# Another choice of the quads whose operand sets are stored ahead of the down projection

## The chip, the cores and the metric

The kernel runs on one core of one Trainium2 chip. The metric is the time of one execution on the device in microseconds (us); the median of several runs is compared. A second number is the span of one execution that the hardware profiler recorded, from which all views below come. Engines: PE is TensorE (matmul), DVE is VectorE, ACT is ScalarE, POOL is GpSimd, SP is SyncE, which issues nearly all transfers here and waits in its order for what each of them needs.

## The reference

One decoder layer in float32 for 256 tokens of width 2048. What matters here is its second half, a gated feed-forward net of width 5632:

```
x = x + concat(attention, pooling) @ w_out
h = rms_norm(x, g)
u = h @ w_up                              # 2048 -> 2 * 5632
y = conv_b + sum of conv_w[i] * u shifted by 2-i tokens, i = 0..2
gate, val = split(y)
out = x + (silu(gate) * val) @ w_down     # 5632 -> 2048
```

## The kernel before

All weights are read once, in 1 MB chunks of 128 x 2048 float32, through four buffers (`raw`). The program is a list of steps; a step uses half a chunk (128 x 1024), so chunk c serves steps 2c and 2c + 1. Each float32 operand is split into a high part `wh` (ACT, L165) and a low part `wl` (DVE, L170), and three matmuls (high x high, high x low, low x high) stand for one exact one. The split of a step is made five steps ahead of its use (`AHEAD`), and when the last split of a chunk is made, its buffer goes to the next load (`release`, L139). The order of all instructions is the order of the program; nothing reorders them.

The feed-forward net is done in thirds of 8, 8 and 6 groups of 256 hidden features. Each third has an up projection (8 steps a group, into `ps_feat`; the convolution and gate follow on DVE, ACT and POOL) and then a down projection over the third's hidden features, made as two pairs (`down_pair`): pair 0 makes output columns 0 to 1023, pair 1 columns 1024 to 2047. A pair has 8 or 6 quads of two steps; quad j uses steps 2j and 2j + 1 of its pair. `MIXED` names for each pair the quads that are made with seven block products in place of eight, in the manner of Strassen and Winograd. A mixed quad needs sums of weight blocks: DVE forms them (L189, L190, L191), and ACT and DVE split them (L211, L213, L224) into an operand set of two tiles `s1` and `s4` (together 128 x 3072, 1.5 MB), and a third sum, t13, is split as an ordinary half chunk.

There are two buffers for sets. Set 0 lies in memory that is kept. Set 1 lies in the memory of the temporaries of the convolution (`temps`), and is opened by `open_temps(True)` in step 2 of a third's pair 0; the last operation that reads one of those temporaries is L761, in the same step. `SECOND` names the quads that use set 1, the other mixed ones use set 0. In pair 0 of the last third the partial results of the mixed quads are taken out of PSUM behind the last mixed quad by `add_part`'s L927, L905, L906 and L910; in the other pairs by L918 to L927.

Two quads of each third do not have their set made in the down projection. Their chunk is loaded once more in the up projection (`extra`, L143), the set is formed there in set 0's memory, and set and t13 are stored to HBM (`early_store`, L204 and L205). In the down projection t13 comes with the chunk's other half (L136, L137), and the set is loaded by `load_set` (L208), `ahead` steps ahead of the quad's first step. `STORED` names these quads by third size, as (pair, quad, ahead):

```
MIXED = {8: ((0, 3, 5, 6), (0, 3, 5, 6)), 6: ((0, 3, 4), (0, 2, 3))}
SECOND = {8: ((5,), (0, 3, 6)), 6: ((4,), (2,))}
STORED = {8: ((0, 6, 4), (1, 5, 6)), 6: ((1, 2, 6), (1, 3, 4))}
...
        for i, (b, j, ahead) in enumerate(STORED[nq]):
            u = u0 + 8 * nq + b * 2 * nq + 2 * j
            at = u0 + 22 + 2 * nq * i - 4 * i * (nq < 8)
            extra[(at + 4) // 2] = u // 2
            after(at, early_sums)
            after(at + 1, early_split)
            after(at + 3, lambda c=u // 2: early_store(c))
            after(u - ahead, lambda c=u // 2, i=int(j in SECOND[nq][b]): load_set(c, i))
```

`after(u, f)` runs f behind step u. In most steps the splits (and so the release of a chunk and the next load) stand ahead of the step's matmuls, and the functions of `after` behind them.

Of the kernel before, what the change touches and what calls it, by code (L numbers as in the profile page):

```python
# [56 lines left out]
THIRDS = ((0, 8), (8, 16), (16, 22))  # L57
MIXED = {8: ((0, 3, 5, 6), (0, 3, 5, 6)), 6: ((0, 3, 4), (0, 2, 3))}
SECOND = {8: ((5,), (0, 3, 6)), 6: ((4,), (2,))}
STORED = {8: ((0, 6, 4), (1, 5, 6)), 6: ((1, 2, 6), (1, 3, 4))}  # L60
SUMMED = {n: sorted(set(a + b)) for n, (a, b) in MIXED.items()}
OUT_MIXED = (2, 3, 5, 6)
OUT_SECOND = (3, 6)
# [25 lines left out]
def layer(ctx: ExitStack, tc: tile.TileContext, xT, xtok, wts, par, rel_d, ident_d, icnt_d, out):  # L89
# [991 lines left out]
    for n, (g0, g1) in enumerate(THIRDS):  # L1081
        nq, u0 = g1 - g0, len(steps)
        for i, (b, j, ahead) in enumerate(STORED[nq]):
            u = u0 + 8 * nq + b * 2 * nq + 2 * j
# [133 lines left out]
```

## Time and profile before

| | |
|---|---|
| median of 3 runs | 1032.47 us (1032.01 to 1034.42) |
| profiled execution | 1034.1 us, span 1032.3 us |
| TensorE busy | 1011.9 us (98%) |
| VectorE busy | 856.8 us (83%) |
| ScalarE busy | 590.5 us (57%) |
| read from HBM, written | 211.56 MB, 15.07 MB |
| down projections (pair 0's first quad) begin at | 469.1, 736.1 and 958.1 us |

A timeline's row gives the start, the duration, the engine, the line and operation, what is written from what, and how many; in brackets stands the idle time of the engine ahead of it and what ended it. In the chain of waits, a row gives start, duration and what. A row of a table by stretches has the stretch, its length, busy time of PE, PE's weight loads, DVE, ACT and POOL, then the granted TensorE clock (1.00 is full), the share of the DMA engines' time and GB/s.

### The profile page before, as it was taken

How to read it: one execution, taken by the hardware profiler on the slowest of the kernel's cores; microseconds unless marked ns; L12 is line 12 of the kernel's file. 1: busy time of each engine (PE TensorE's matmuls, PEld its weight loads, DVE VectorE, ACT ScalarE, POOL GpSimd, SP SyncE). 2: the span in 40 equal slices, each digit the busy share in tenths (PEclk: the TensorE clock that was granted, in tenths of full speed). 3: DMA queues.
4: the chain of work that ended last, by engine and by line, in shares of the span. 5: the costliest groups of instructions: out<-in, count | busy, mean ns of one | idle time of the engine just before them, and what ended most of it. 6: DMA issues, size and time to landing. Idle time of an engine off the chain costs nothing.

```text
span 1032.3 us, 13718 instructions
## 1 busy us (share of the span) xinstructions
PE 1011.9 (98%) x5229; PEld 865.0 (84%) x5229; DVE 856.8 (83%) x1105; ACT 590.5 (57%) x803; POOL 102.5 (10%) x110
## 2 busy tenths in 40 slices
PE   9999999999999999999899999999989999999988
PEld 8788888888888888888688888888868888888766
DVE  5998767888988888889785898898987679888984
ACT  6855664565666655655455555665555465555561
POOL 0220005500001111000000111100000001110011
PEclk9999999999999999999899999999999999999999
DMA  9784553475554585845587647685476775577476
GB/s 334 283 263 177 194 184 120 163 305 183 206 201 165 204 317 185 317 168 197 224 306 221 228 172 273 216 320 200 163 284 202 290 225 183 195 290 291 163 242 207
DMA packets 36801, 233.81 MB, mean 226 GB/s; under 512 B 4264, under 2 KB 5160, under 8 KB 12416
## 3 DMA queue, kind: packets, MB, share of 16 engines
q1 hardware_dynamic: 34000, 224.15, 59.7%
q0 software_dynamic: 2736, 8.78, 4.2%
q8 instruction: 41, 0.67, 0.3%
q14 instruction: 24, 0.20, 0.1%
HBM read 211.56 MB, written 15.07 MB: 220 GB/s over the span
## 4 chain that ended last, share of the span: by engine, by line
PE 91%; DVE 4%; DMA 3%; issue 1%; ACT 1%; SPq 0%; DVEq 0%; ACTq 0%
PE ps_feat L251 33%; PE ps_feat L253 17%; PE ps_down L866 14%; PE ps_tok L238 8%; PE ps_p L806 7%; PE ps_down L806 5%; DMA s<-s 3%; PE ps_v L245 3%; DVE wl L170 2%; PE ps_pool L260 1%; PE ps_s L468 1%; ACT wh L165 0%; PE ps_start L313 0%; PE ps_down L888 0%; DVE y L735 0%
## 5 line engine op out<-in xcount | busy, mean ns | idle before, releaser
L170 DVE TENSOR_TENSOR wl<-raw,wh 128x1024 fp32r<-128x1024 f32 x358 | 441.6, 1247 | 85.2 <-ACT wh L165 28.5
L251 PE MATMUL ps_feat<-x2h,wh 128*128 128x512 f32 x1408 | 488.8, 392 | 0.0
L165 ACT ACTIVATE wh<-raw 128x1024 fp32r<-128x1024 f32 x358 | 369.2, 1051 | 123.1 <-DVE raw L189 67.7
L253 PE MATMUL ps_feat<-x2h,wl 128*128 128x256 f32 x1408 | 393.5, 280 | 0.0
L251 PEld LDWEIGHTS ps_feat<-x2h,wh 128*128 128x128 f32 x1408 | 264.2, 188 | 58.4
L253 PEld LDWEIGHTS ps_feat<-x2h,wl 128*128 128x128 f32 x1408 | 264.2, 188 | 0.1
L730 ACT ACTIVATE y<-fs,pv 128x256 f32<-128x256 f32 x88 | 48.2, 595 | 64.5 <-DVE fs L728 64.5
L735 DVE SCALAR_TENSOR_TENSOR y<-fs,pv,y 128x255 f32<-128x255 f32 (+1 forms) x176 | 81.0, 481 | 3.2
L866 PE MATMUL ps_down<-wh,hid 128*128 128x512 f32 x336 | 83.1, 389 | 0.0
L866 PEld LDWEIGHTS ps_down<-wh,hid 128*128 128x128 f32 x336 | 63.1, 188 | 13.4
L780 POOL TENSOR_TENSOR s<-y 128x128 f32<-128x128 f32 x24 | 32.6, 1358 | 349.0 <-DVE y L754 349.0
L211 ACT ACTIVATE s<-raw 128x512 fp32r<-128x512 f32 (+1 forms) x54 | 45.4, 840 | 17.5 <-DVE raw L191 14.9
L896 POOL DMA_DIRECT2D x<-st x13 | 11.5, 921 | 408.5 <-ACT st L971 329.0
L251 PE MATMUL ps_feat<-xh,wh 128*128 128x512 f32 x128 | 46.3, 402 | 0.0
L866 PE MATMUL ps_down<-wl,hid 128*128 128x512 f32 x168 | 44.9, 389 | 0.0
L520 ACT ACTIVATE fs<-ps_feat 128x512 f32<-128x512 f32 (+1 forms) x46 | 26.2, 570 | 21.8 <-PE ps_feat L253 21.8
L866 PEld LDWEIGHTS ps_down<-wl,hid 128*128 128x128 f32 x168 | 31.5, 188 | 6.6
L755 ACT ACTIVATE hid<-y 128x512 fp32r<-128x512 f32 x22 | 13.9, 634 | 38.5 <-DVE y L754 38.5
L253 PE MATMUL ps_feat<-xh,wl 128*128 128x256 f32 x128 | 35.8, 280 | 0.0
L238 PE MATMUL ps_tok<-wh,xh 128*128 128x512 f32 x128 | 35.5, 399 | 0.0
L806 PE MATMUL ps_p<-wh,sx 128*128 128x512 f32 x104 | 34.6, 415 | 0.0
L245 PE MATMUL ps_v<-wh,xh 128*128 128x512 f32 x128 | 34.5, 391 | 0.0
(240 smaller groups left out, 1271.7 us busy)
## 6 DMA issues: line engine op xcount, KB each, us to landing
raw<-in_wts SPq DMA_DIRECT2D x177, 1024.0 KB, 5.0
s<-s SPq DMA_DIRECT2D x12, 1536.0 KB, 11.6
x<-st POOLq DMA_DIRECT2D x11, 512.0 KB, 9.0
raw<-in_wts SPq DMA_DIRECT2D x10, 512.0 KB, 5.4
t<-t SPq DMA_DIRECT2D x6, 512.0 KB, 9.5
raw<-t SPq DMA_DIRECT2D x6, 512.0 KB, 5.8
x<-in_xtok SPq DMA_DIRECT2D x1, 2048.0 KB, 9.2
raw<-in_wts SPq DMA_DIRECT2D x7, 256.0 KB, 5.6
```

The costliest lines, as they stand in the source:

```text
L165: nc.scalar.activation(wparts[u][0], raw(u - 1 if u - 1 in seven else u + 1 if u in seven else u), AF.Copy)
L170: nc.vector.tensor_tensor(wl, raw(u - 1 if u - 1 in seven else u + 1 if u in seven else u), wh.bitcast(F32), op=OP.subtract)
L211: nc.scalar.activation(parts[0], w, AF.Copy)
L238: nc.tensor.matmul(ps[:, t, :], act[:, k0 + k, a, t * P:(t + 1) * P], w[:, k * 512:(k + 1) * 512], start=(first and k == 0 and n == 0), st ...
L245: nc.tensor.matmul(ps[:, t, :], act[:, k, a, t * P:(t + 1) * P], w[i], start=(first and n == 0), stop=(last and n == 2))
L251: nc.tensor.matmul(ps, wh[:, ws], act[:, k, :, :], start=(first and n == 0), stop=False, skip_group_check=True)
L253: nc.tensor.matmul(ps[:, S:], wl[:, ws], act[:, k, 0, :], start=False, stop=(last and n == len(ks) - 1), skip_group_check=True)
L730: nc.scalar.activation(y[:, m, :], u[:, m, :], AF.Identity, scale=cw[m][2], bias=col(C_CB + f0_ + m))
L735: nc.vector.scalar_tensor_tensor(y[:, m, d:], u[:, m, :S - d], cw[m][2 - d], y[:, m, d:], op0=OP.mult, op1=OP.add)
L780: eng.tensor_tensor(s[:, n, :], a, b, op=op)
L806: nc.tensor.matmul(ps, act[a], w[i], start=(first and n == 0), stop=(last and n == 2), skip_group_check=skip)
L866: nc.tensor.matmul(bank(t, b), hid(order[j] + h, t)[a], part(w, b if h == 0 else 1 - b)[i], start=(n == 0 and h == 0 and (fresh or j == no ...
```

## The change

In the thirds of eight quads, the first stored quad of pair 0 is quad 5 in place of quad 6, with its load seven steps ahead in place of four; quad 5 uses set 1, quad 6 set 0. Quad 5 of pair 1 stays stored. In the last third, quad 4 of pair 0 and quad 2 of pair 1 (both set 1) are stored, in place of quads 2 and 3 of pair 1, with loads five and six steps ahead. The sets of quad 6 (thirds of eight) and of quad 3 of pair 1 (last third) are now made in the down projection. Each engine has as many instructions as before.

```
-STORED = {8: ((0, 6, 4), (1, 5, 6)), 6: ((1, 2, 6), (1, 3, 4))}
+STORED = {8: ((0, 5, 7), (1, 5, 6)), 6: ((0, 4, 5), (1, 2, 6))}
```

SP in pair 0 of the first third, before and after: `raw` are chunks, `t` a stored t13, `s_1926` set 0, `s_4352` set 1, and `s_3315` the stored set in HBM.

```order
-L139 DMA raw<-in_wts 128x2048 x11
+L139 DMA raw<-in_wts 128x2048 x10
 L136 DMA raw<-in_wts 128x1024
 L137 DMA raw<-t_3314 128x1024
-L139 DMA raw<-in_wts 128x2048 x4
-L208 DMA s_1926<-s_3315 128x3072
 L139 DMA raw<-in_wts 128x2048 x2
+L208 DMA s_4352<-s_3315 128x3072
+L139 DMA raw<-in_wts 128x2048 x5
```

The load of the stored set has moved ahead past three chunk loads, from behind chunk 10's to behind chunk 7's (chunks counted from the pair's first), and into the other buffer. The second third changes in the same way.

SP in the last third, before; `s_8443` is set 1, `s_7554` set 0:

```order
L139 DMA raw<-in_wts 128x2048 x9
L136 DMA raw<-in_wts 128x1024
L137 DMA raw<-t_7798 128x1024
L136 DMA raw<-in_wts 128x1024
L137 DMA raw<-t_8014 128x1024
L139 DMA raw<-in_wts 128x2048
L208 DMA s_8443<-s_7799 128x3072
L139 DMA raw<-in_wts 128x2048
L208 DMA s_7554<-s_8015 128x3072
```

And after, where `s_8444` is set 1:

```order
L139 DMA raw<-in_wts 128x2048 x5
L136 DMA raw<-in_wts 128x1024
L137 DMA raw<-t_7798 128x1024
L139 DMA raw<-in_wts 128x2048 x3
L208 DMA s_8444<-s_7799 128x3072
L136 DMA raw<-in_wts 128x1024
L137 DMA raw<-t_8014 128x1024
L139 DMA raw<-in_wts 128x2048 x2
L208 DMA s_8444<-s_8015 128x3072
L139 DMA raw<-in_wts 128x2048
```

Both loads now go into set 1; the first stands behind the load of pair 1's second chunk.

DVE in the last third, from L761 (step 2 of pair 0) to the removal of pair 0's partial results, before:

```order
L761 TENSOR_TENSOR hid<-y,hid 128x2x256
L170 TENSOR_TENSOR wl<-raw,wh 128x1024
L213 TENSOR_TENSOR s_8443<-raw,s_8443 128x512
L189 TENSOR_TENSOR raw<-raw 128x1024
L190 TENSOR_TENSOR raw<-raw 128x512
L191 TENSOR_TENSOR raw<-raw 128x512
L170 TENSOR_TENSOR wl<-raw,wh 128x1024
L224 TENSOR_TENSOR s_8443<-raw,s_8443 128x1024
L170 TENSOR_TENSOR wl<-raw,wh 128x1024 x3
L213 TENSOR_TENSOR s_7554<-raw,s_7554 128x512
```

And after:

```order
L761 TENSOR_TENSOR hid<-y,hid 128x2x256
L170 TENSOR_TENSOR wl<-raw,wh 128x1024 x5
L213 TENSOR_TENSOR s_7554<-raw,s_7554 128x512
L189 TENSOR_TENSOR raw<-raw 128x1024
L190 TENSOR_TENSOR raw<-raw 128x512
L191 TENSOR_TENSOR raw<-raw 128x512
L170 TENSOR_TENSOR wl<-raw,wh 128x1024
L224 TENSOR_TENSOR s_7554<-raw,s_7554 128x1024
L170 TENSOR_TENSOR wl<-raw,wh 128x1024
L927 TENSOR_TENSOR x_1923<-ps_p_8368,x_1923 128x2x512
L906 TENSOR_TENSOR st<-ps_p,st 128x512
```

The making of quad 4's set, in `s_8443`, is gone from between the splits; the set in `s_7554` that follows is that of pair 1's first quad in both.

## The prediction

> **What bounds the kernel now.** I read the page first, then the waits, the chain, and the timelines of TensorE, VectorE and SP around each wait that the chain names. The page gives the span and TensorE's share.
>
> ```profile
> span 1032.3 us, 13718 instructions
> PE 1011.9 (98%) x5229; PEld 865.0 (84%) x5229; DVE 856.8 (83%) x1105; ACT 590.5 (57%) x803; POOL 102.5 (10%) x110
> ```
>
> TensorE is the bound; only its 20 us of idleness, and the slow clock behind a stop, can be won without touching its work. Two rows of the waits (total, times, longest) name stops inside the down projections:
>
> ```profile
> PE ps_p L806 <- DMA s<-s: 8.7, 3, 4.2
> PE ps_p L806 <- DVE st L906: 3.8, 1, 3.8
> ```
>
> Three stops wait for a load of a stored set, the first two over 3.8 us each. The chain shows why they are late (start, duration, what):
>
> ```profile
> 494.11 0.33 SPq L139
> 494.49 9.66 DMA s<-s
> ...
> 761.50 9.26 DMA s<-s
> ```
>
> The set for quad 6 of pair 0 is issued at 494.49 and lands 9.66 us later. TensorE's timeline gives what it costs; the rows are the starts of quads 5, 6 and 7 of pair 0 in the first third, of quads 5 and 7 of its pair 1 (where no stop is), and of quads 5 and 7 of pair 0 in the second third.
>
> ```profile
> 494.99 0.86 PE L806 MATMUL ps_p<-s,hid 128*128 128x512 f32 x3
> ...
> 504.20 1.65 PE L806 MATMUL ps_p<-s,hid 128*128 128x512 f32 x3 [4.19 <-DMA s<-s]
> ...
> 511.96 1.98 PE L866 MATMUL ps_down<-wh,hid 128*128 128x512 f32 x8
> ...
> 543.48 0.84 PE L806 MATMUL ps_p<-s,hid 128*128 128x512 f32 x3
> ...
> 553.10 2.00 PE L866 MATMUL ps_down<-wh,hid 128*128 128x512 f32 x8
> ...
> 761.93 0.86 PE L806 MATMUL ps_p<-s,hid 128*128 128x512 f32 x3
> ...
> 778.41 1.75 PE L866 MATMUL ps_down<-wh,hid 128*128 128x512 f32 x7
> ```
>
> Two mixed quads take 553.10 - 543.48 = 9.62 us undisturbed, 4.81 each. In pair 0 they take 511.96 - 494.99 = 16.97 and 778.41 - 761.93 = 16.48. The stop therefore costs 7.35 us in the first third and 6.86 in the second, 14.2 in all. Of the first, 4.40 is idleness (504.20 less quad 5's end, 494.99 + 4.81 = 499.80) and 2.95 slow matmuls: the granted clock (third value from the end) is 0.60 in the stretch behind it.
>
> ```profile
> 499.90:504.20 4.30, 0.11 (x2) 0.00 (x1) 4.16 (x5) 3.06 (x3) 0.00 (x0) 0.92 0.98 414
> 504.20:512.00 7.80, 7.80 (x22) 6.16 (x23) 2.93 (x4) 2.57 (x4) 0.00 (x0) 0.60 0.49 181
> ```
>
> **Part 1, the thirds of eight quads: the load is moved to quad 5.** Its buffer is set 1, which no quad of pair 0 uses before. It lies in the temporaries' memory, so its load (step 3, right behind chunk 7's) waits for their last reader, VectorE's L761. The rows give that L761 in the first and second third, chunk 7's issue (the first of the four), and the times from issue to landing of all six loads of sets:
>
> ```profile
> 482.06 0.68 DVE L761 TENSOR_TENSOR hid<-y,hid 128x512 fp32r<-128x512 f32 x1
> 749.01 0.69 DVE L761 TENSOR_TENSOR hid<-y,hid 128x512 fp32r<-128x512 f32 x1
> 482.17 12.27 SPq L139 DMA_DIRECT2D raw<-in_wts  x4
> DMA to landing us min/median/max: 8.6/9.3/10.9
> ```
>
> Issue is at 482.8 and 749.75. With the longest landing, 10.9, the sets are there at 493.7 and 760.7; quad 5 needs them at 494.99 and 761.93. The margin is 1.3 us at worst. The load now shares the DMA engines with chunk 7 ahead and chunks 8 and 9 behind: 3 x 1.05 + 1.57 = 4.72 MB. At the 414 GB/s of the row above all of it is in 11.4 us after 482.17, at 493.6, so even equal sharing doesn't make it late. I take a gain of 14.2 us.
>
> A rule of the Trainium skill speaks against this: "DMA: Bandwidth & Descriptors", section "Where 436 GB/s comes from", says that for transfers between HBM and SBUF about 358 GB/s bind. By it the 4.72 MB would take an estimated 13.2 us, the set could come at 495.4, and the sum below would be 0.8 us worse. The trace's 414 GB/s is above that limit, so I keep the row.
>
> **Part 2, quad 6's set is now made there.** The same five VectorE operations (L213, L189, L190, L191, L224) leave quad 5 and join quad 6. In the last third one such set with a split (L170) in it lies between these rows:
>
> ```profile
> 977.77 0.69 DVE L213 TENSOR_TENSOR s<-raw,s 128x512 fp32r<-128x512 f32 x1
> ...
> 983.45 3.49 DVE L170 TENSOR_TENSOR wl<-raw,wh 128x1024 fp32r<-128x1024 f32 x3
> ```
>
> That is 5.68 us with one split of 1.16, so 4.5 without. In the first third VectorE comes from L761 at 482.74, makes five splits (to 488.5) and the set (to 494.2). Quad 6 starts at 494.99 + 4.81 = 499.8, and quad 3 has left set 0 by 494.99 - 5.44 = 489.55, where quad 4 starts (an unmixed quad takes 5.44, see part 3). The cover is 5.6 us; cost 0. Bytes, DMA counts, and ACT's copies stay equal.
>
> **Part 3, the turn to pair 1.** Without the stop, quad 0 of pair 1 starts at 494.99 + 9.62 + 5.44 = 510.05 instead of 517.40 (5.44 is quad 7, 511.96 to 517.40). It overwrites the bank that L924 reads. VectorE's and ACT's rows there, and the old start:
>
> ```profile
> 503.07 1.23 DVE L224 TENSOR_TENSOR s<-raw,s 128x1024 fp32r<-128x1024 f32 x1
> 510.35 0.70 DVE L919 TENSOR_TENSOR ps_p<-ps_p,s 128x512 f32<-128x512 f32 x1 [0.63 <-ACT s L918]
> 513.15 1.22 DVE L924 TENSOR_TENSOR x<-ps_p,x 128x1024 f32<-128x1024 f32 x1
> 501.98 1.06 ACT L211 ACTIVATE s<-raw 128x1024 fp32r<-128x1024 f32 x1 [0.40 <-DVE raw L191]
> 508.07 1.06 ACT L165 ACTIVATE wh<-raw 128x1024 fp32r<-128x1024 f32 x1 [4.09 <-PE ps_p L806]
> 509.72 0.60 ACT L918 ACTIVATE s<-ps_p 128x512 f32<-128x512 f32 x1 [0.59 <-PE ps_p L806]
> 517.40 0.86 PE L806 MATMUL ps_p<-s,hid 128*128 128x512 f32 x3
> ```
>
> ACT is free at 503.04, makes two copies (1.0 each) and L918 (0.6): 505.6. VectorE is through L224 at 504.3 and a split at 505.5. L919 thus starts at 505.65, and L924 ends 513.15 + 1.22 - 510.35 = 4.02 later, at 509.7: 0.35 us before it is needed. The old slack was 3.0. I put the cost at 0, with up to 1 us in each third as the other end, since nothing is idle in this count.
>
> **Part 4, the last third.** Quad 4 of pair 0 becomes a stored one; its load stands at step 3, five steps ahead. But here VectorE is late:
>
> ```profile
> 976.03 0.69 DVE L761 TENSOR_TENSOR hid<-y,hid 128x512 fp32r<-128x512 f32 x1
> 976.81 0.63 ACT L211 ACTIVATE s<-raw 128x512 fp32r<-128x512 f32 x1 [1.01 <-DVE hid L761]
> 939.91 36.56 SPq L139 DMA_DIRECT2D raw<-in_wts  x7
> ...
> 981.10 0.86 PE L806 MATMUL ps_p<-s,hid 128*128 128x512 f32 x3
> ...
> 994.65 1.92 ACT L971 ACTIVATE st<-ps_down 128x1024 f32<-128x1024 f32 x2
> 995.61 1.65 PE L806 MATMUL ps_p<-s,hid 128*128 128x512 f32 x3 [3.79 <-DVE st L906]
> ...
> 1001.87 1.98 PE L866 MATMUL ps_down<-wh,hid 128*128 128x512 f32 x8
> ...
> 1012.96 0.97 PE L806 MATMUL ps_p<-s,hid 128*128 128x512 f32 x3 [0.63 <-DMA s<-s]
> ...
> 1018.03 5.44 PE ps_down L866 x24
> ```
>
> Set 1 is free at 976.72: ACT's first write into it waited for the same L761. Quad 4 starts at 981.10, 4.4 us later, and no set lands in under 8.6. A chunk is issued just ahead (976.14, the last of seven), as at 494.11, so I take 9.5: the set lands at 986.25, quad 4 is 5.15 us late, and the clock drops; the nearest stop in length (4.40 us) lost 2.95 by it. Quads 4 and 5 end at 986.25 + 4.81 + 5.44 + 2.95 = 999.4, where quad 0 of pair 1 used to start at 995.61.
>
> The Trainium skill, "TensorE: Matmul & The Clock Gate", Part 1 on the HAM clock gate, has the half rate end after one busy window of about 3.4 us. One such window would lose an estimated 1.7 us, and the sum below would be 1.2 us better. The trace lost 2.95 behind the stop of this length, and the row is kept.
>
> What goes in exchange: VectorE makes one set less (4.5 us) ahead of L906, the cause of the 3.79 us stop. L906 now follows quad 4's first half (986.25 + 2.4, and some 1.5 of slow clock: 990) and two of VectorE's operations, near 993 by my estimate; so that stop is gone and so is its slow clock (quad 0 took 6.26 instead of 4.81). Quad 3 of pair 1, no longer stored, loses its wait of 0.63. Its set is made once ACT has evicted pair 0's banks (1.92 us from 999.4) and made two copies, from about 1004 to 1011, before 1014.4. Pair 1's one stored set has 15 us, from quad 4's end (994) to quad 2 (1009.6). So quads 0 to 3 run through: 999.4 + 3 x 4.81 + 5.44 = 1019.3 (quad 3's end), against 1018.03 before. The last third is 1.2 us longer. Its ends: landing 8.6 and the 1.45 of clock that the 3.79 us stop cost give 1.1 shorter; 10.9 and 0.5 more of clock give 3.1 longer.
>
> **Sum.** -14.2 + 0 + 0 + 1.2 = -13.0. The profiled execution took 1034.1 (span 1032.3), so it would take 1021.1; the runs' median, 1032.47, is 1.6 below that execution, and I predict 1019.5.
>
> **Rivals.** The turn to pair 1 becomes the bound (part 3): L924 late by 1 to 2.5 us in both thirds, at full clock. For it: the slack of 0.35 us. Against it: VectorE and ACT are waiting, not working, at 508 to 510 today. It gives about 1019.5 + 3 = 1022.5. Chance 0.15.
>
> Quad 5's set is late. It decides from a landing of 12.2 us on, beyond the longest load. One late by a microsecond in both thirds gives 1021.5. A short stop keeps the clock up, as behind this one of 2.24 us:
>
> ```profile
> 964.65 0.96 PE L806 MATMUL ps_down<-s,hid 128*128 128x512 f32 x3 [2.24 <-DVE fs L524]
> 964.70:968.00 3.30, 3.30 (x15) 2.73 (x16) 3.23 (x6) 2.05 (x3) 0.00 (x0) 1.00 0.63 204
> ```
>
> Chance 0.10.
>
> The last third doesn't stop, and its old losses go: 3.8 and 1.45 at quad 0, and 1.1 at quad 3 (1018.03 less 1001.87 + 5.44 + 2 x 4.81): 1032.47 - 14.2 - 6.3 = 1012. Against it stand the 976.72 and the 8.6. Chance 0.05.
>
> Slower: SP issues in order, and a set's load that waits for its buffer holds all weight chunks behind it. If set 1 were free only 10 us after L761, sets would land near 502, and quad 5 would stop as quad 6 does now, with the last third's new stop longer by as much: about 1032.5 + 1.2 + 10 = 1043. Only from about 6 us on does this eat the gain. Against it: ACT wrote into set 1 at 976.81, 0.1 us behind L761. Chance 0.02. That the stops move without changing the time (a gain eaten at the turn and in the last third together) has 0.02.
>
> **Numbers.** The forecast has 0.66. Its own ends are 2.3 below (last third) and 1.9 + 2 above (last third, turns): 1017.2 to 1023.4. The rivals of the turn and of quad 5 lie inside that; with a little room for the base, whose runs differ by 2.4, the range is 1016.0 to 1024.0. About 0.3% (3 us) is what a measurement of this kernel can tell from no change; all cases but the last two rivals are beyond it: faster 0.95, same 0.03, slower 0.02.
>
> **What would show it.** Right: no wait of quad 6 for a set in the first two thirds, quad 5 to quad 7 in 9.6 to 9.7 us, the granted clock at 1.00 there; set 1's load issued within 0.2 us of L761; one new stop of about 5 us at quad 4 in the last third, with slow matmuls behind it, and none for L906. Wrong: a stop at the start of pair 1 with VectorE's L924 or L927 as releaser, a stop at quad 5, or SP held at the set's load while chunks are wanted.

## The result, and the profile after

The changed kernel takes 1019.0 us (median of 4 runs, 1017.68 to 1019.69), the kernel before 1032.59 us on the same chip (4 runs, 1032.01 to 1034.42). The ratio is 0.9864, with a 95% interval from 0.9847 to 0.9881: by it 14 us less (12.3 to 15.8). The forecast was 1019.5. The profiled execution took 1018.5 us.

The page's first lines, to be laid beside those of before:

```profile
span 1016.7 us, 13717 instructions
PE 1007.4 (99%) x5229; PEld 863.0 (85%) x5229; DVE 855.8 (84%) x1105; ACT 589.0 (58%) x803; POOL 102.4 (10%) x110
```

The span is 15.6 us shorter, and only 4.5 of that is TensorE's busy time (1011.9 to 1007.4); the rest was idleness. The waits of TensorE in the down projections (total, times, longest):

```profile
PE ps_down L806 <- DVE fs L524: 2.2, 1, 2.2
...
PE ps_p L806 <- DMA s<-s: 1.9, 1, 1.9
```

Of three waits for a stored set, 8.7 us together, one is left with 1.9 us. The one for L906 (3.8 us) is gone. The one for L524, inside the last third's first quad, was there before with the same 2.2 us.

TensorE's timeline has the starts of quads 5, 6 and 7 of pair 0 and of pair 1's first quad in the first third, then those of quads 5, 6 and 7 in the second:

```profile
494.80 0.86 PE L806 MATMUL ps_p<-s,hid 128*128 128x512 f32 x3
...
499.66 0.85 PE L806 MATMUL ps_p<-s,hid 128*128 128x512 f32 x3
...
504.44 1.98 PE L866 MATMUL ps_down<-wh,hid 128*128 128x512 f32 x8
...
509.88 0.86 PE L806 MATMUL ps_p<-s,hid 128*128 128x512 f32 x3
...
754.41 0.86 PE L806 MATMUL ps_p<-s,hid 128*128 128x512 f32 x3
...
759.27 0.85 PE L806 MATMUL ps_p<-s,hid 128*128 128x512 f32 x3
...
764.05 1.98 PE L866 MATMUL ps_down<-wh,hid 128*128 128x512 f32 x8
```

No row has a bracket: nothing waits. Quads 5 and 6 take 504.44 - 494.80 = 9.64 us, and 764.05 - 754.41 = 9.64 again, where they took 16.97 and 16.48. The stretch behind quad 6's start has the full clock (third value from the end), where it had 0.60:

```profile
499.60:504.40 4.80, 4.80 (x22) 3.95 (x22) 4.68 (x6) 3.69 (x4) 0.00 (x0) 1.00 0.25 102
```

SP's timeline gives the issue of chunk 7 and of set 1's load in the first third; the view of L208 gives the times from issue to landing of the loads of sets:

```profile
481.98 0.33 SPq L139 DMA_DIRECT2D raw<-in_wts  x1
482.64 0.33 SPq L208 DMA_DIRECT2D s<-s  x1
```

```profile
DMA to landing us min/median/max: 7.9/9.0/10.4
```

That view has five of the six loads; the one at 482.64 is not among them, and the same load of the second third landed after 9.0 us. Even with the longest landing the set would be there at 482.64 + 10.4 = 493.0, 1.8 us ahead of quad 5.

In the last third stand the first quad (943.78), its second half behind the wait for L524 (950.26), then quads 3, 4 and 5 of pair 0 and quad 0 of pair 1:

```profile
943.78 0.86 PE L806 MATMUL ps_p<-s,hid 128*128 128x512 f32 x3
...
950.26 0.98 PE L806 MATMUL ps_down<-s,hid 128*128 128x512 f32 x3 [2.22 <-DVE fs L524]
951.08 3.27 PE L866 MATMUL ps_down<-wh,hid 128*128 128x512 f32 x8
...
963.61 0.84 PE L806 MATMUL ps_p<-s,hid 128*128 128x512 f32 x3
...
970.47 0.94 PE L806 MATMUL ps_p<-s,hid 128*128 128x512 f32 x3 [1.94 <-DMA s<-s]
...
976.96 2.00 PE L866 MATMUL ps_down<-wh,hid 128*128 128x512 f32 x8
...
982.42 0.84 PE L806 MATMUL ps_p<-s,hid 128*128 128x512 f32 x3
```

The chain of waits has the load that quad 4 waited for, and the unmixed quad that starts where quad 3 of pair 1 ends, as at 1018.03 before:

```profile
962.41 7.92 DMA s<-s
...
1002.42 5.44 PE ps_down L866 x24
```

From 943.78 to 1002.42 are 58.64 us; before it was 1018.03 - 958.14 = 59.89. (The chain puts the start of such a quad 0.16 us later than TensorE's timeline, in both profiles alike.) So in these two profiles 7.33 + 6.84 = 14.17 us went in the thirds of eight quads, 1.25 in the last third, and 0.2 ahead of them.

### The profile page after: what moved, and what is told of

Read it like the earlier page. It is cut to its first block, busy times and chain, and to the rows that moved or that the text cites. A ratio compares the mean times of both kernels' runs of the same rounds, so it can differ in the third digit from the quotient of the medians.

```text
span 1016.7 us, 13717 instructions
## 1 busy us (share of the span) xinstructions
PE 1007.4 (99%) x5229; PEld 863.0 (85%) x5229; DVE 855.8 (84%) x1105; ACT 589.0 (58%) x803; POOL 102.4 (10%) x110
## 4 chain that ended last, share of the span: by engine, by line
PE 90%; DVE 4%; DMA 3%; ACT 1%; issue 1%; SPq 0%; DVEq 0%; ACTq 0%
PE ps_feat L251 34%; PE ps_feat L253 17%; PE ps_down L866 15%; PE ps_tok L238 9%; PE ps_p L806 7%; PE ps_down L806 6%; DMA raw<-in_wts 2%; DVE wl L170 1%; DMA s<-s 1%; ACT wh L165 1%; PE ps_pool L260 1%; DVE y L735 1%; PE ps_s L468 1%; PE ps_down L888 0%; PE ps_T L455 0%
## 5 line engine op out<-in xcount | busy, mean ns | idle before, releaser
L238 PE MATMUL ps_tok<-wh,cat 128*128 128x512 f32 x128 | 34.4, 390 | 0.0
```

The source lines that it names most:

```text
L238: nc.tensor.matmul(ps[:, t, :], act[:, k0 + k, a, t * P:(t + 1) * P], w[:, k * 512:(k + 1) * 512], start=(first and k == 0 and n == 0), st ...
```

## The experiments

All change one line, `STORED`, of the kernel before. A minus line is that of the kernel before, a plus line the experiment's. Times are medians, each beside runs of the kernel before on the same chip.

**The thirds of eight quads alone.**

```
-STORED = {8: ((0, 6, 4), (1, 5, 6)), 6: ((1, 2, 6), (1, 3, 4))}
+STORED = {8: ((0, 5, 7), (1, 5, 6)), 6: ((1, 2, 6), (1, 3, 4))}
```

> The new choice in the thirds of eight quads alone; the last third stays as before. By the theory (the gain is the two stops of quad 6, 7.3 + 6.9 us) this kernel takes the 14.2 us off the kernel before: 1018.3, ratio 0.986. By the forecast's part 4 (the last third's change costs 1.2) it is 1.2 faster than the full change; by the trace of the full change (its last third is 58.5 us against 59.9 before) it is 1.4 slower than the full change. The rival, that the last third's change brings a large part of the gain, expects 1025 or more. The profile should show no wait of quad 6 for a set in the first two thirds, and the old stops in the last: about 2.2 us inside quad 0, 3.8 behind L906, 0.6 at quad 3 of pair 1.

Measured: 1018.79 us (4 runs, 1018.2 to 1019.13) against 1031.76, ratio 0.9874 (0.9861 to 0.9887): 13.0 us less, by the interval 11.7 to 14.3. Within the intervals that is the whole gain of the change. In its last third TensorE's stops are these:

```profile
948.95 0.97 PE L806 MATMUL ps_down<-s,hid 128*128 128x512 f32 x3 [2.22 <-DVE fs L524]
...
979.89 0.97 PE L806 MATMUL ps_p<-s,hid 128*128 128x512 f32 x3 [2.36 <-DVE st L906]
...
997.07 0.97 PE L806 MATMUL ps_p<-s,hid 128*128 128x512 f32 x3 [0.18 <-DMA s<-s]
```

The program there is that of before, and still the stops for L906 and for quad 3's set are shorter (2.36 against 3.79, 0.18 against 0.63). TensorE came to pair 1 35.1 us behind the first quad's start (979.89 - 2.36 - 942.46), and 33.7 before (995.61 - 3.79 - 958.14), while L906 let it go at the same 37.4 to 37.5. The repeats below show what had held it up.

**The last third alone.**

```
-STORED = {8: ((0, 6, 4), (1, 5, 6)), 6: ((1, 2, 6), (1, 3, 4))}
+STORED = {8: ((0, 6, 4), (1, 5, 6)), 6: ((0, 4, 5), (1, 2, 6))}
```

> The new choice in the last third alone; the thirds of eight stay as before. The forecast's part 4 expects 1.2 us more than before: 1033.7, ratio 1.001. The trace of the full change expects 1.4 us less: 1031.2, ratio 0.9986. Both expect the two stops of quad 6 (about 4.2 us each, with slow matmuls behind). The rival that the last third's change carries the gain expects under 1025. The stop inside quad 0 of the last third (2.2 us) should be there again; if the clock behind it depends on where the stop falls in time, the slow matmuls behind it may or may not come with it.

Measured: 1032.35 us (12 runs, 1029.46 to 1033.77), ratio 1.0003 (0.9993 to 1.0013) to the same 1031.76: by the ratio 0.3 us more, by the interval from 0.7 less to 1.3 more. No gain or loss of this part is shown; the 1.2 us more of the forecast lie inside the interval, the 1.25 us less of the changed kernel's profile outside it. Its stops for a set, quad 6's two and the new one at quad 4:

```profile
502.90 0.95 PE L806 MATMUL ps_p<-s,hid 128*128 128x512 f32 x3 [3.43 <-DMA s<-s]
...
768.23 1.65 PE L806 MATMUL ps_p<-s,hid 128*128 128x512 f32 x3 [3.85 <-DMA s<-s]
...
982.93 1.62 PE L806 MATMUL ps_p<-s,hid 128*128 128x512 f32 x3 [4.32 <-DMA s<-s]
```

Here the stop at quad 4 is 4.3 us long, near the 5.15 of the forecast; in the changed kernel's profile the same stop was 1.9.

**The set's load four steps and five steps later** (quad 5 as in the change, `ahead` 3 and 2 in place of 7; the last third as in the change). VectorE's order is that of the changed kernel in both, so that the load's place is all that differs.

```
-STORED = {8: ((0, 6, 4), (1, 5, 6)), 6: ((1, 2, 6), (1, 3, 4))}
+STORED = {8: ((0, 5, 3), (1, 5, 6)), 6: ((0, 4, 5), (1, 2, 6))}
```

> The full change, but in the thirds of eight the load of quad 5's set stands three steps ahead in place of seven: SP issues it behind chunk 9, some 4.9 us later. VectorE's order is the same as in the full change. Theory (the time from issue to landing against the time to quad 5 is what counts): issue near 487.5 for a quad due at 494.8, landing 9.0 to 10.4 later, so quad 5 stops for 1.7 to 3.1 us in each of the two thirds, and loses 0 to 1.7 more by the clock: 1022.4 to 1028.6. Rival (the gain came from where VectorE makes the sets, the load is hidden anyway): 1019, no wait for a set at quad 5.

```
-STORED = {8: ((0, 6, 4), (1, 5, 6)), 6: ((1, 2, 6), (1, 3, 4))}
+STORED = {8: ((0, 5, 2), (1, 5, 6)), 6: ((0, 4, 5), (1, 2, 6))}
```

> The full change, but in the thirds of eight the load of quad 5's set stands two steps ahead, behind chunk 10, where the load of quad 6's set stood before the change. VectorE's order is the same as in the full change. Theory: issue near 494.3 for a quad due at 494.8, so quad 5 stops for 8.3 to 9.7 us in each of the two thirds and loses 1.6 to 3 more by the clock: 1039 to 1044, slower than before the change. Rival (where VectorE makes the sets brings the gain): 1019.

Measured: 1025.38 us with three steps (6 runs, 1020.25 to 1026.85), ratio 0.9931 (0.9913 to 0.9949); 1038.7 us with two (3 runs, 1037.11 to 1039.02; before: 1032.06), ratio 1.0059 (1.0036 to 1.0082). So with the one place of the load the kernel is 6 to 7 us slower than the changed one, and with the other 20 us. The profiled execution with three steps was among the faster of its six, at 1023.9 us. The load's issue with three steps, and quad 5's stops in the first and second third:

```profile
486.80 0.38 SPq L208 DMA_DIRECT2D s<-s  x1
```

```profile
496.68 0.94 PE L806 MATMUL ps_p<-s,hid 128*128 128x512 f32 x3 [2.46 <-DMA s<-s]
...
758.25 0.93 PE L806 MATMUL ps_p<-s,hid 128*128 128x512 f32 x3 [1.72 <-DMA s<-s]
```

And with two steps:

```profile
494.22 0.38 SPq L208 DMA_DIRECT2D s<-s  x1
```

```profile
502.50 1.62 PE L806 MATMUL ps_p<-s,hid 128*128 128x512 f32 x3 [7.75 <-DMA s<-s]
...
771.95 1.62 PE L806 MATMUL ps_p<-s,hid 128*128 128x512 f32 x3 [7.82 <-DMA s<-s]
```

Issue plus the load's own 8.1 to 9.7 us of landing gives the start of quad 5 to within 0.2 us each time. What counts is the lead in microseconds; storing another quad gains nothing by itself.

**The first quad of the last third in place of quad 4.** The thirds of eight are as in the change. Quad 0's set is loaded eight steps ahead of it, still in the up projection, into the memory that is kept; quad 4's set is made in the down projection.

```
-STORED = {8: ((0, 6, 4), (1, 5, 6)), 6: ((1, 2, 6), (1, 3, 4))}
+STORED = {8: ((0, 5, 7), (1, 5, 6)), 6: ((0, 0, 8), (1, 2, 6))}
```

> The full change in the thirds of eight; in the last third the stored quads are quad 0 of pair 0 (set 0, loaded eight steps ahead, in the up projection) and quad 2 of pair 1. VectorE then makes one set less just where it is latest (ahead of the last third's first quad), and quad 4's set is made as before the change. Theory (the last third's stops all come from VectorE being 4 to 5 us late at its start): the stop inside quad 0 (2.2 us and 1.6 of clock in the trace of the full change) and the one at quad 4 (2.05 and 1.7) go, L906 is in time: 7.6 us less than the full change, 1011.4. Rival: one of them is only moved; L906 late again as before the change (3.8 us and 1.5 of clock) gives about 1016; the stop inside quad 0 staying (because it waits for the convolution and not for the set) gives 1015.

Measured: 1013.87 us (4 runs, 1012.36 to 1014.19), ratio 0.9824 (0.9811 to 0.9837). By the medians it is 5 us better than the change, by the ratios 4, and 2.5 slower than the 1011.4 that I had expected. The waits for L524 and at quad 4 are gone from TensorE's list; what is left is one stop at the start of pair 1, for L906:

```profile
976.07 0.97 PE L806 MATMUL ps_p<-s,hid 128*128 128x512 f32 x3 [2.19 <-DVE st L906]
```

L906 does come sooner, 33.1 us behind the first quad's start (976.07 - 942.96) where it was 37.5 before, and for TensorE's old arrival at 33.7 that would have been enough. But TensorE, no longer held for 2.2 us in quad 0, arrives at 30.9.

**No set that is late.** The first quad is stored as above, and with it quad 3 of pair 0 in place of quad 2 of pair 1, which takes a set's making from VectorE ahead of L906.

```
-STORED = {8: ((0, 6, 4), (1, 5, 6)), 6: ((1, 2, 6), (1, 3, 4))}
+STORED = {8: ((0, 5, 7), (1, 5, 6)), 6: ((0, 0, 8), (0, 3, 5))}
```

> The full change in the thirds of eight; in the last third the stored quads are quads 0 and 3 of pair 0, both in set 0: quad 0 loaded eight steps ahead, quad 3 five steps ahead, right behind quad 0's last use of set 0. VectorE then makes two sets less ahead of L906 than before the change, and three sets in pair 1. Theory: every stop of the last third comes from VectorE's lateness there or from a load with less than 9 to 10 us to its quad; quad 3's load has 10.9 us (947.75 to 958.63 in the trace of the kernel with quads 0 and 2 stored), L906 is done 2 us before it is needed, so no stop is left: about 50.6 us from the last third's first quad to the end of quad 3 of pair 1, in place of 54.7, which gives about 1010. Rival: the stop moves into pair 1, where VectorE now makes three sets (counted: quad 3's s4 ready 1 to 2 us before use), or quad 3 waits for its set; each of 2 us and 0 to 1.7 of clock gives 1012 to 1014.

Measured: 1009.46 us (5 runs, 1009.32 to 1010.16), ratio 0.9781 (0.9761 to 0.9801): 22.6 us less than before, the fastest of the versions measured here. The page and the longest wait of TensorE, which is the one at the program's start:

```profile
span 1007.7 us, 13715 instructions
PE 1003.3 (100%) x5229; PEld 861.0 (85%) x5229; DVE 855.7 (85%) x1105; ACT 588.9 (58%) x803; POOL 103.3 (10%) x110
```

```profile
PE ps_start L313 <- DVE ones L310: 1.1, 1, 1.1
```

No stop is left in any down projection. The last third's stretch that took 58.64 us in the changed kernel takes 993.42 - 942.67 = 50.75 by the same two rows; 50.6 was expected.

**The changed kernel twice more**, one execution each, to see what its last third does without any change of the program.

```
-STORED = {8: ((0, 6, 4), (1, 5, 6)), 6: ((1, 2, 6), (1, 3, 4))}
+STORED = {8: ((0, 5, 7), (1, 5, 6)), 6: ((0, 4, 5), (1, 2, 6))}
```

> The changed kernel once more, for the stop of 2.2 us inside the last third's first quad. In five traces the two quads behind it took 10.9 us (the kernel before, and two experiments) or 12.5 us (the changed kernel, and one experiment). If the program decides which, this run shows 12.5 again, with a stop of about 1.9 us at quad 4. If it is a matter of where the stop falls against the clock's own periods, it may show 10.9, and then a stop of 4.3 us at quad 4.

> As the run before it, a second time: 12.5 us and 1.9 us if the program decides, either pair (12.5 and 1.9, or 10.9 and 4.3) if it does not.

Measured: 1018.56 and 1019.42 us. In the first repeat, TensorE behind the wait for L524, at quad 3 and at quad 4, and the stretch behind the first of these:

```profile
949.78 1.65 PE L806 MATMUL ps_down<-s,hid 128*128 128x512 f32 x3 [2.24 <-DVE fs L524]
...
963.06 0.84 PE L806 MATMUL ps_p<-s,hid 128*128 128x512 f32 x3
...
970.70 1.62 PE L806 MATMUL ps_p<-s,hid 128*128 128x512 f32 x3 [2.71 <-DMA s<-s]
```

```profile
949.80:956.00 6.20, 6.20 (x20) 5.04 (x21) 5.95 (x9) 3.20 (x5) 0.00 (x0) 0.72 0.69 255
```

And the same in the second repeat:

```profile
949.62 0.98 PE L806 MATMUL ps_down<-s,hid 128*128 128x512 f32 x3 [2.24 <-DVE fs L524]
...
961.35 0.84 PE L806 MATMUL ps_p<-s,hid 128*128 128x512 f32 x3
...
970.23 1.62 PE L806 MATMUL ps_p<-s,hid 128*128 128x512 f32 x3 [3.96 <-DMA s<-s]
```

```profile
949.60:956.00 6.40, 6.38 (x28) 5.26 (x29) 6.12 (x10) 3.20 (x5) 0.00 (x0) 1.00 0.69 256
```

The stop of 2.24 us is the same in both. Behind it the granted clock falls to 0.72 in the one (963.06 - 949.78 = 13.28 us to quad 3) and stays at 1.00 in the other (11.73). Where TensorE has lost 1.55 us there, it comes to quad 4 later and waits less for the set: 2.71 against 3.96. Behind quad 4's stop the shorter wait costs less as well: quad 4 took 6.30 us in the one (970.70 to 977.00) and 7.69 in the other (970.23 to 977.92). So the loss behind the first stop is more than taken back at the second, and the repeat that had it was the faster of the two.

## Why the prediction was right, and where it was not

**Part 1 (14.2 us from the thirds of eight quads): right.** The part alone timed 13.0 us with an interval that reaches 14.3. The 14.17 us of the two profiles show that the stops are gone, but are no second measurement of their size: they take the same two times of before, 16.97 and 16.48, as the forecast. Those are one draw. In the profile of the last third alone, where these thirds are as before, quads 5 and 6 took 509.39 - 494.45 = 14.94 and 775.81 - 759.35 = 16.46, by which the stops cost 12.1 us. The steps hold one by one: set 1's load was issued right behind L761, at 482.64 (forecast 482.8), the landing in the second third was 9.0 us (the forecast's "all six" landings were five, for its view too lacks one), and the clock was full. The two later loads show that the lead is the cause: the quad's choice was kept, the load was put 4.9 and 11.8 us later in the first third (counted from the pair's first quad, which starts at 468.92, 468.17 and 468.70), and quad 5 stopped for 2.5 and 7.8 us.

The rule on the DMA engines that was weighed there ("DMA: Bandwidth & Descriptors", section "Where 436 GB/s comes from", of the Trainium skill) would have put the set at an estimated 495.4 and a short stop at quad 5. TensorE has none at 494.80, and the longest landing ends at 493.0; the changed kernel's transfers ran at 430 GB/s from 486 to 490 and at 426 from 490 to 494, so the trace's rate of 414 GB/s was the one to work with.

**Part 2 (quad 6's set made in place, at no cost): right.** VectorE's last operation for the set, L224, ends at 493.99 (forecast 494.2), quad 6 begins at 499.66 without a wait, and no other wait on VectorE has come up in these thirds.

**Part 3 (the turn to pair 1): right, and as narrow as said.** L924 of the first third:

```profile
508.04 1.22 DVE L924 TENSOR_TENSOR x<-ps_p,x 128x1024 f32<-128x1024 f32 x1
```

It ends at 509.26, and pair 1 begins at 509.88: a slack of 0.62 us where 0.35 was forecast. The rival by which the turn becomes the bound decides only beyond that, and did not come.

**Part 4 (the last third 1.2 us longer): the mechanism was right, the size was not.** Quad 4 did stop for its set, the clock did fall, the stop for L906 did go, and no stop is left in pair 1. But against the 1.2 us longer of the forecast the last third was 1.25 us shorter in the profiled execution, and 0.3 longer in the timed comparison of this part alone, whose interval the 1.2 just fits. (The forecast set 1019.3, a sum of timeline rows, against the chain's 1018.03; against the timeline's 1017.87 its own sum is 1.4.) Three terms were off:

- The landing was taken at 9.5 us. It was 7.9 here, and 8.3 to 8.7 in the five other profiles with this load behind L761 (the two repeats, the last third alone, the load at three steps and at two).
- "A short stop keeps the clock up" was the step that failed. The prediction had it from one row, the 2.24 us stop for L524, behind which the clock was 1.00, and so put the slow clock behind this stop at nothing. The same stop cost 13.35 - 11.69 = 1.66 us in the changed kernel's profile (950.26 to 963.61, against 964.65 to 976.34 before). That is not a loss on top: it comes ahead of quad 4, whose need for the set it puts off. VectorE's L761, which opens set 1, does not move with it:

```profile
961.64 0.68 DVE L761 TENSOR_TENSOR hid<-y,hid 128x512 fp32r<-128x512 f32 x1
```

  It starts 11.38 us behind the end of the first stop, as before (961.64 - 950.26 and 976.03 - 964.65), but quad 3 now starts 1.97 us behind L761 and started 0.31 behind it before (976.34 - 976.03). So the stop at quad 4 came out at about 2 us (5.15 forecast); with the clock up at that point it is 4.0 to 4.3 us, in the second repeat, in the last third alone and at three steps.
- The slow clock behind quad 4's stop was taken at 2.95 us, from a stop of 4.4 (4.19 by its bracket). It was 6.49 - 4.81 = 1.68 behind the stop of 1.9 (970.47 to 976.96), and 7.69 - 4.81 = 2.9 behind the one of 3.96.

The 2.4 us that the last third was off in the profile are in large part a draw. From the first quad to the unmixed quad behind quad 3 of pair 1, both by TensorE's timeline, the six profiles with this last third took 58.5, 59.0 and 59.2 us where the clock fell behind the stop for L524, and 60.0, 60.1 and 60.4 where it did not. The two with the old last third took 59.5 (it fell) and 59.7 (it did not). So the forecast's sign holds in the branch that it assumed, with 0.3 to 0.7 us, and not in the other.

That the sum came within 0.5 us of the median is luck in part. The timed difference between medians is 13.6 us where 13.0 was summed, but taken alone part 1 gave 1.2 us less than its 14.2, and part 4 cost 0.9 less than its 1.2: the two misses offset each other, and both are smaller than the intervals resolve.

The Trainium skill, "TensorE: Matmul & The Clock Gate", Part 1 on the HAM clock gate, states windows of about 3.4 us that run freely, half rate after an idle one, and full rate after a busy one. One window at half rate would lose an estimated 1.7 us; the losses of 1.5 to 1.7 us agree, and windows that run freely would explain why the same stop costs once nothing and once 1.6. Two things do not fit: stops of 1.9 and 2.2 us, shorter than such a window, lowered the clock, and those of 3.85 to 4.3 us lost 2.5 to 2.95, more than those of 7.8 us with 1.9 to 2.0.

The rivals with a set that is late at quad 5, or held back by its buffer, were not borne out in the changed kernel; the load at three and at two steps shows what a late set costs there: 1025.4 us where it was late by 1.7 and 2.5 us in the profile, and 1038.7 where it was late by 7.8.

What stays open: what decides which of the two outcomes an execution gets. No run here isolates it; the outcome can be read only afterwards, from the timeline.

## What to carry to other kernels

The lead of a load is to be counted in microseconds from when its buffer is free to when the data are wanted, against the landings of the trace (8 to 11 us for these 1.5 MB); a quad with that lead gained 14 us, and one that was five steps ahead with a lead of 4 to 6 us gained nothing. When a stop is taken away, everything behind it is wanted sooner by as much, so the next wait is to be worked out for the earlier time: with the first quad stored, its stop of 2.2 us was gone and one of 2.2 us stood at the start of pair 1, until VectorE was relieved there as well. A term that rests on the clock behind one stop in one profile is a draw between two outcomes, and belongs into the range with both.

## What the runs showed of the hardware

The clock behind a stop was not set by the stop's length alone. The loss is the time of the mixed quad behind the stop less 4.81 us (for the stop for L524, the time to quad 3 less 11.69):

| stop of TensorE, us | lost by the slow clock, us |
|---|---|
| 1.7 and 2.5 (load at three steps) | 0.1 and 0.1 |
| 1.9 (quad 4, changed kernel) | 1.7 |
| 2.2 (L524, eight profiles) | 0 in four, 1.6 to 1.7 in four |
| 2.2 and 2.4 (L906, with the first quad stored; thirds of eight alone) | 1.7 and 1.7 |
| 2.7 (quad 4, first repeat and load at two steps) | 1.5 and 1.7 |
| 3.4 (quad 6, last third alone) | 1.7 |
| 3.8 (L906, before) | 1.45 |
| 3.85 (quad 6, before and last third alone) | 2.8 and 2.8 |
| 4.0 to 4.3 (four stops for sets) | 2.5 to 2.95 |
| 7.75 and 7.8 (load at two steps) | 1.9 and 2.0 |

The four profiles that lost nothing at L524 are those of before, of the last third alone, of the load at three steps and of the second repeat. The program's kind does not sort them, since the changed kernel stands on both sides.

The spread of the runs fits this: the kernel without stops has a granted clock of 1.000 and its five runs lie within 0.84 us, while the kernel before spread over 6.1 us in ten runs on the same chip.
